# A one-core decoder layer: fewer side matmuls for denominators, first norm and HGRN2 row copies

## The chip, the cores and the metric

The kernel runs on one core of one Trainium2 chip. The metric is the device time of one execution in microseconds (us). Before the change the median of three runs was 2330.41 us (2330.23 to 2330.99).

## The reference

One layer of a decoder is computed for two groups of tokens that share the weights: one new sequence of 256 tokens, and 8 sequences of 8 tokens each that continue from a stored state (64 tokens). All 320 tokens go through every weight matrix together. In short:

```
proj = x @ w_in                      # 2048 -> 16392 columns
A: mLSTM, 4 heads:  s = (q k^T) * decay;  num = s v + q C0;  den = sum_s s + q n0
   h = num / max(|den|, exp(-m));  normalised per head
   C_new = decay * C0 + sum_s w_s k_s v_s^T
B: HGRN2, 8 heads:  o = (decayed q k^T) v + (q * decay) S0;  S_new = decay * S0 + sum_s k'_s v_s^T
x1 = LayerNorm(alpha*x + W_out(sig(ga)*A W_a + sig(gb)*B W_b))
y  = LayerNorm(alpha*x1 + relu(x1 W_up)^2 W_down)
```

Two sums matter here. `den` is a row sum of the score matrix, one number per token. The LayerNorm needs, for each token, the sum and the sum of squares over 2048 channels. And one update matters: for each of the 8 sample sequences, the state S of each HGRN2 head gets the sum over 8 tokens of a key row times a value row.

## The kernel before, in words

**Main stream.** Activations lie as channels x tokens: 16 blocks of 128 channels, 320 tokens wide. The weights are cut into 304 tiles of 2048 x 128. A tile is 16 steps, and each step is three matmuls, since each fp32 value is split into a high and a low fp32r part (high x high, high x low, low x high). That is 14592 matmuls of 320 columns. A half tile (512 KB, "unit") is loaded by SP into one of three raw buffers `wr`; ScalarE makes the high part (`wh`, line 331), VectorE the low part (`wl`, line 480), into three pairs of buffers; later tiles use five more pairs in `bb`.

**Side work.** Everything else is put between main steps by a planner that runs when the program is built. Pieces of work are Python generators ("chains") that yield (engine, cost, function). The planner keeps a clock for each engine; a PE piece is placed into TensorE's stream only once the planner believes that its operands are there (450 ns after the last of them, `PE_LAT`, and 140 ns more for a change of engine, `LAT`). A transfer costs SP 620 ns in the plan. The order is fixed then; on the chip each engine runs its own stream in order and waits on semaphores. So a wrong belief about a time turns into a wait of the whole stream behind that piece.

**The places that the change touches.**

- mLSTM scores (`m_S`, line 855) leave the masked scores of the prompt in the tile E, in three blocks of 128 columns; blocks 2 and 3 belong to the same 128 tokens. `m_num` (line 1008) sums them over s by matmuls with a column of ones, `one`, in fp32: one for the first 128 tokens, two that accumulate for the second. `m_sample` (line 1071) does the same for the sample tokens with three such matmuls: one over E, two over qn (q times the stored n0, two halves of the 256 channels).
- HGRN2 values (`h_i`, line 1374): the values of the 64 sample tokens are transposed, then split into a high part (partitions 64 to 127 of `vst`) and a low part (0 to 63). For the update each sequence needs its 8 rows four times, as high, high, low, low, at 32 partitions of its own. Two fp32r matmuls of 256 columns with a 0/1 matrix `spread` copy the rows into a PSUM bank, and ScalarE copies the bank back into `vst`.
- HGRN2 keys (`h_state`, line 1420): after a VectorE product, `stack` (line 915) writes high and low parts four times over into 256 columns (one ScalarE, one VectorE instruction), two transposes (line 1441) turn the two groups of 128 columns, and ScalarE copies them to `kst`.
- `h_update` (line 1469) waits for `vst`, takes four PSUM banks, issues eight matmuls of 32 rows x 256 columns, then eight VectorE instructions update the state tiles, and SP stores them. `hkst` and `hvst` are pools of one buffer, freed after the update.
- First LayerNorm (n = 0) and second (n = 1): `ln_sum` adds each block into S1 and its square into S2 on VectorE. After block 14 `ln_pre` (line 1717) starts two fp32 matmuls of a 128 x 128 matrix of ones with S1 and S2 (320 columns each); `ln_final` (line 1724) adds block 15 and its square to the same banks by two more.

**Order.** mLSTM heads 0 to 3 run in the first 440 us or so; the HGRN2 heads between about 440 and 850 us, one for each six tiles; then branches, output projection (16 tiles, the first norm at its end), and the feed-forward tiles. SP issues nearly all transfers in one in-order stream, the weight reloads among them.

Of the kernel before, what the change touches and what calls it, by code (L numbers as in the profile page):

```python
# [232 lines left out]
def wait(*evs):  # L233
    return ("wait", evs)
# [10 lines left out]
def post(ev):  # L245
    return ("set", ev)


def act(n, psum=False, ptr=0):
    return ((61 if psum else 112) + n) / 1.2 + 93 * ptr  # L250


def dve(n, psum=False, mode=1, ptr=0):
    return ((62 if psum else 66) + n / mode) / 0.96 + 55 * ptr
# [39 lines left out]
class Program:  # L294
# [48 lines left out]
    def carve(self):  # L343
        class Part:
            def __init__(self, ap, lo=0):
                self.ap, self.o, self.end = ap, lo, ap.shape[1]

            def __call__(self, n, parts=128):
                self.o += n
                assert self.o <= self.end, (self.o, self.end)  # L350
                return self.ap[:parts, self.o - n:self.o]

            def three(self, a, b):
                return self(a * b).rearrange("p (a b) -> p a b", a=a)

        self.Part = Part
        A, B, C, R = Part(self.f1), Part(self.f2), Part(self.f3), Part(self.ra[:, 0:6400])

        self.hs = Pool([A(2048) for _ in range(3)])

        self.qk = Pool([A.three(4, 320) for _ in range(2)])
        self.vr = Pool([A.three(4, 320)])
        self.kw = Pool([B.three(2, 320)])
        self.bc = Pool([B(712) for _ in range(2)])
        self.eb0 = B(512)
        self.eb = Pool([self.eb0])
        self.stg = Pool([B(256) for _ in range(2)])
        self.qn0 = B(256)
        self.qn = Pool([self.qn0])
        X = Part(self.rx)  # L370
        self.cb = Pool([C(512) for _ in range(6)] + [X(512) for _ in range(8)])
        self.hb = Pool([C.three(3, 512)])
        self.qz0 = C(512)
        self.qz = Pool([self.qz0])
        self.tst = Pool([B(320) for _ in range(2)])
        self.tst2 = B(320)
        self.shl = Pool([(R(384), R(384), R(256))])
        self.vhl = Pool([R(2048).rearrange("p (x s v) -> p x s v", x=2, s=2)])
        self.vs = Pool([R(512)])
        self.khl = Pool([R(1024).rearrange("p (x s k) -> p x s k", x=2, s=2)])  # L380
        self.kst = Pool([R.three(2, 256)])
        self.vst = Pool([R.three(2, 512)])

        A, B, R = Part(self.f1, 6144), Part(self.f2), Part(self.rh)
        self.sb = Pool([A.three(4, 256) for _ in range(2)])
        self.at = Pool([A(512) for _ in range(2)])
        self.yb0 = A(1024)
        self.yb = Pool([self.yb0])
        self.it2 = [B.three(3, 256) for _ in range(2)]
        self.it = Pool(self.it2)  # L390
        self.hstg = Pool([B(256) for _ in range(2)])
        self.on0 = B.three(3, 256)
        self.on = Pool([self.on0])
        self.ho = Pool([B(320) for _ in range(2)])
        R2 = Part(self.ra, 5120)
        self.hkst = Pool([R2.three(2, 128)])
        self.phl = Pool([(R2(512), R2(512))])
        self.hvst = Pool([R.three(2, 256)])
        self.late = [B(320) for _ in range(4)]
        self.ats0 = B(128)  # L400
        self.ats = Pool([self.ats0])
        self.sg = Pool([Part(self.f2, 4960)(320), self.tst2])
        B = Part(self.f2, 4304)
        self.sr = Pool([B(320) for _ in range(2)])
        B = Part(self.f2, 3840)
        self.xr = Pool([B(320) for _ in range(4)])
        B = Part(self.f2)
        self.lnb = [B(320) for _ in range(7)]
        self.tmp = Pool([B(320) for _ in range(3)])

    def carve_h(self):
# [3 lines left out]
        pp = C(512)  # L415
        self.pp = Pool([pp])
        self.ktk = Pool([C.three(2, 128)])
        for x in (qz, self.ats0, pp[:, 480:512], self.yb0[:, 320:384], *(y[64:128, 2, :] for y in self.it2)):
            self.nc.gpsimd.memset(x, 0.0)
        X, R = self.Part(self.pool.tile([128, 4096], F32R, name="rxb", tag="rx")), self.Part(self.ra)  # L420
        self.bah = Slices([(X if j < 12 else R)(TOK) for j in range(KT)])
# [436 lines left out]
    def m_S(self, h):  # L858
# [21 lines left out]
        yield ("dve", dve(384), lambda: v.tensor_tensor(sl, E[:, 0:384], f(sh), ALU.subtract))  # L880
        yield ("dve", dve(128), lambda: v.tensor_tensor(ss[64:128, 128:256], E[64:128, 384:512], f(ss[64:128, 0:128]), ALU.subtract))
        yield ("act", act(256), lambda: self.A(ss[0:64], f(ss[64:128])))
        yield post(m["S"])

    def m_V(self, h):
# [31 lines left out]
    def stack(self, st, src, his):  # L917

        v = self.nc.vector
        w = st.rearrange("p (b r t) -> p b r t", r=4, t=8)  # L920
        x = src.rearrange("p (b t) -> p b t", t=8).unsqueeze(2).to_broadcast([128, 8, 2, 8])
        step = his[1] - his[0]
        los = [r for r in range(4) if r not in his]
        pick = lambda rs: w[:, :, rs[0]:rs[0] + 2 * step - (step - 1):step, :]
        hi, lo = pick(his), pick(los)
        yield ("act", act(128), lambda: self.A(hi.bitcast(F32R), x))
        yield ("dve", dve(128), lambda: v.tensor_tensor(lo.bitcast(F32R), x, hi, ALU.subtract))

    def m_KW(self, h):
        nc, v, m = self.nc, self.nc.vector, self.mh[h]  # L930
# [78 lines left out]
    def m_num(self, h):  # L1009
# [9 lines left out]
        db = yield acq(self.sbank)  # L1019
        m["db"] = db  # L1020
        one = self.one
        yield ("pe", 212, lambda: self.mm(db[:, 0:1], E[:, 0:128], one, start=True, stop=True))
        yield ("pe", 212, lambda: self.mm(db[:, 1:2], E[:, 128:256], one, start=True, stop=False))
        yield ("pe", 212, lambda: self.mm(db[:, 1:2], E[:, 256:384], one, start=False, stop=True))
        for i in range(2):
            b = yield acq(self.sbank)
            jobs = [(c, s) for c, s in (((0, 0),), ((128, 0), (256, 1)))[i]]
# [50 lines left out]
    def m_sample(self, h):  # L1078
# [27 lines left out]
        for i in range(2):  # L1106
            yield ("pe", pe_r(512), lambda: self.mm(nb, ss[:, 128 * i:128 * i + 128], m["vs"], start=False, stop=i == 1, skip_group_check=True))
        db = yield acq(self.sbank)
        yield ("pe", 212, lambda: self.mm(db[:, 0:1], E[:, 384:512], self.one, start=True, stop=False))
        for c in range(2):  # L1110
            yield ("pe", 212, lambda: self.mm(db[:, 0:1], qn[:, 128 * c:128 * c + 128], self.one, start=False, stop=c == 1))
        dn = yield acq(self.sm)
        yield ("dve", 80, lambda: v.tensor_copy(dn[:, 0:1], db[:, 0:1]))
        yield rel(self.sbank, db)
# [81 lines left out]
    def h_start(self, h):  # L1196
# [2 lines left out]
        a = m["set"] = self.hs.free.pop(0)[1]  # L1199
        a = self.Part(a)  # L1200
        m["qk"], m["fs"], m["iv"] = a.three(2, 384), a.three(2, 320), a.three(2, 320)
        for n in ("f", "q", "lv", "o", "pre8", "suf", "I", "SP", "S", "aT", "qz", "ist", "sdone", "got", "ld"):
            m[n] = Ev()
        m["i"] = [Ev(), Ev()]
        m["Y"] = [Ev() for _ in range(5)]
# [165 lines left out]
    def h_i(self, h):  # L1371
# [22 lines left out]
        yield ("dve", dve(256, True), lambda: v.tensor_tensor(lo, b[64:128, 0:256], hi.bitcast(F32), ALU.subtract))  # L1394
        yield rel(self.sbank, b)
        yield post(m["I"])
        b = yield acq(self.sbank)
        bv = b.rearrange("p (g k) -> p g k", g=2)
        for g in range(2):
            yield ("pe", pe_r(256), lambda: self.mm(bv[:, g, :], self.spread[:, g, :], vst[:, 0, :], start=True, stop=True))  # L1400
        yield ("act", act(512, True), lambda: self.A(vst, bv))
        yield rel(self.sbank, b)
        yield post(m["ist"])

    def h_load(self, h):

# [13 lines left out]
    def h_state(self, h):  # L1420
# [10 lines left out]
            cap(qz, 0, [[136, 2], [32, 4], [1, 8]]), by_token(qk[:, 1, :], 256, False), by_token(fs[:, 1, :], 256, False), ALU.mult))  # L1431
        sm = yield acq(self.sm)
        yield ("dve", 80, lambda: v.tensor_copy(sm[:, 0:8], sv(fs[:, 1, :])[:, :, 7]))
        ks = fs[:, 0, 256:320]
        yield ("dve", dve(64), lambda: v.tensor_tensor(ks, qk[:, 0, 256:320], ks, ALU.mult))
        kst = yield acq(self.hkst)
        b = yield acq(self.sbank)
        st = yield acq(self.hstg)
        yield from self.stack(st, ks, (0, 2))
        for g in range(2):  # L1440
            yield ("pe", PE_T, lambda: nc.tensor.transpose(b[:, 128 * g:128 * g + 128], st[:, 128 * g:128 * g + 128], self.ident))  # L1441
        yield rel(self.hstg, st)
        yield ("act", act(256, True), lambda: self.A(kst, b[:, 0:256].rearrange("p (g k) -> p g k", g=2)))
        yield rel(self.sbank, b)
        ob = yield acq(self.sbank)
        m["ob2"] = ob
        yield wait(m["ld"])
# [21 lines left out]
    def h_update(self, h, kst, sm, e):  # L1469

        v, m = self.nc.vector, self.hh[h]
        yield wait(m["ist"])
        vst = m["vst"]
        ps = yield acq(self.sbank, 4)
        yield ("pe", PE_4 + 2 * pe_r(256), lambda: [self.mm(
# [192 lines left out]
    def ln_add(self, n, j, z, pre):  # L1668
# [29 lines left out]
            return  # L1698
        yield from self.ln_sum(j, z)
        yield post(st["s"][j])  # L1700
        if j == 14:
            self.s.spawn(self.ln_pre(n), 0)

    def ln_sum(self, j, z):
# [19 lines left out]
    def ln_final(self, n, z):  # L1724
# [3 lines left out]
        M, RS, X, T = (self.lnb[i] for i in (3, 4, 5, 6))  # L1728
        q = yield acq(self.tmp)
        t = yield ("act", act(TOK), lambda: self.A(q, z, AF.Square))  # L1730
        yield wait(st["pre"])
        p1, p2 = (p[:, :TOK] for p in st["p"])
        yield ("pe", pe_f(TOK), lambda: self.mm(p1, self.ones, z, start=False, stop=True))
        yield ("pe", pe_f(TOK), lambda: self.mm(p2, self.ones, q, start=False, stop=True))
        yield rel(self.tmp, q)
        yield post(st["fin"])
        t = yield ("act", act(TOK, True), lambda: self.A(M, p1, scale=1.0 / D))
# [122 lines left out]
    def run(self, pool):  # L1860
# [8 lines left out]
        self.vx, self.kx, self.main_end = Pool([]), Pool([]), Ev()  # L1869
        self.sD = [self.dr.tile([128, 768], F32, name=f"sD{j}") for j in range(HH)]  # L1870
        self.kD = [self.dr.tile([128, 2, 2, 256], F32, name=f"kD{j}") for j in range(MH)]
        self.vD = [self.dr.tile([128, 2, 2, 512], F32, name=f"vD{j}") for j in range(MH)]
        self.ln = [dict(c=Ev(), end=Ev(), pre=Ev(), m=Ev(), fin=Ev(), s=[Ev() for _ in range(KT)]) for _ in range(2)]
        self.xq, self.xq_ev = [None] * KT, [Ev() for _ in range(KT)]
# [80 lines left out]
```

## Time and profile before

The profiled execution took 2331.78 us; its span from first to last instruction is 2329.7 us.

| what | value |
|---|---|
| median of three runs | 2330.41 us |
| profiled execution, its span | 2331.78 us, 2329.7 us |
| PE (matmul) busy | 2314.0 us, 99% |
| weight loads into PE busy | 2266.9 us, 97% |
| VectorE (DVE) busy | 1381.1 us, 59% |
| ScalarE (ACT) busy | 1048.4 us, 45% |
| hardware DMA queue, share of 16 engines | 51.9% |
| mean granted TensorE clock | 0.999 |

PE is TensorE, DVE is VectorE, ACT is ScalarE, POOL is GpSimd, SP issues transfers. A group of the profile is named by line, engine, operation and tiles (out<-in). Most matmuls have line 337, because one helper issues them; they are told apart by their tiles. Matmuls are pipelined: a record can last about twice the distance between two starts, so costs on PE are read from the distance of starts, not from the length of records. "SPq" is SP's transfer stream.

### The profile page before, as it was taken

To read this page: it belongs to the slowest core of one execution; us is meant where nothing else is said; L and a number is where in the kernel's file an instruction comes from. 1 tells how busy PE (TensorE), PEld (TensorE's weight loads), DVE (VectorE), ACT (ScalarE), POOL (GpSimd) and SP (SyncE) were. 2 spreads that over 40 slices of the span, in tenths; PEclk is the share of its full clock that TensorE was granted. 3 is DMA by queue.
4 is the path that set the end of the run, shared out by engine and by line. 5 is a ranking of instruction groups with operands and counts; after the bars stand their busy time and mean duration, and the time that the engine had idled before them with its cause. 6 is when DMAs were issued, how large, how long until landed. Compare 5 with 4: busy or idle time off the path is not lost.

```text
span 2329.7 us, 38945 instructions
## 1 busy us (share of the span) xinstructions
PE 2314.0 (99%) x15746; PEld 2266.9 (97%) x15746; DVE 1381.1 (59%) x2400; ACT 1048.4 (45%) x1669; POOL 12.7 (1%) x42
## 2 busy tenths in 40 slices
PE   8999999999999999999999999999999999999998
PEld 7999999999999999999999999999999999999998
DVE  5566557677777776555555767544554455445555
ACT  4444445455555565444433446533442344334434
POOL 0000000000000000000000000000000000000000
PEclk9999999999999999999999999999999999999999
DMA  5777766555555554554555644444444444444465
GB/s 201 261 272 264 255 237 228 189 198 187 182 178 184 180 197 172 173 178 170 175 173 172 221 160 144 154 146 153 145 150 149 149 151 146 153 145 152 147 226 181
DMA packets 143580, 424.95 MB, mean 182 GB/s; under 512 B 16412, under 2 KB 37796, under 8 KB 142376
## 3 DMA queue, kind: packets, MB, share of 16 engines
q1 hardware_dynamic: 142248, 416.17, 51.9%
q0 software_dynamic: 1152, 6.29, 0.8%
q8 instruction: 123, 2.02, 0.4%
q14 instruction: 57, 0.47, 0.1%
HBM read 371.50 MB, written 50.90 MB: 181 GB/s over the span
## 4 chain that ended last, share of the span: by engine, by line
PE 97%; DMA 1%; DVE 1%; ACT 0%; issue 0%; SPq 0%; DVEq 0%; ACTq 0%
PE bank L337 96%; DMA wr<-wt 1%; DVE f3m L1844 0%; DVE f3m L1849 0%; PE bank L1553 0%; PE bank L899 0%; PE bank L1125 0%; DVE bb L480 0%; PE bank L1383 0%; ACT bb L331 0%; ACT wh L331 0%; DVE wl L480 0%; SPq L340 0%; PE bank L972 0%; PE bank L1441 0%
## 5 line engine op out<-in xcount | busy, mean ns | idle before, releaser
L480 DVE TENSOR_TENSOR wl<-wr,wh 128x1024 fp32r<-128x1024 f32 (+1 forms) x430 | 525.7, 1223 | 472.6 <-ACT wh L331 464.0
L337 PE MATMUL bank<-xh,wh 128*128 128x320 f32 (+1 forms) x2432 | 790.1, 325 | 0.9 <-ACT wh L331 0.9
L337 PE MATMUL bank<-xh,wl 128*128 128x320 f32 (+1 forms) x2432 | 754.3, 310 | 0.0
L337 PE MATMUL bank<-xl,wh 128*128 128x320 f32 (+1 forms) x2432 | 752.3, 309 | 0.0
L331 ACT ACTIVATE wh<-wr 128x1024 fp32r<-128x1024 f32 (+1 forms) x430 | 453.8, 1055 | 458.1 <-PE bank L337 433.0
L337 PEld LDWEIGHTS bank<-xh,wh 128*128 128x128 f32 x2432 | 458.7, 189 | 21.7 <-issue 15.0
L337 PEld LDWEIGHTS bank<-xl,wh 128*128 128x128 f32 x2432 | 459.5, 189 | 3.5
L337 PEld LDWEIGHTS bank<-xh,wl 128*128 128x128 f32 x2432 | 458.8, 189 | 0.2 <-DVE wl L480 0.2
L480 DVE TENSOR_TENSOR bb<-wr,bb 128x1024 fp32r<-128x1024 f32 x179 | 219.3, 1225 | 237.4 <-ACT bb L331 237.4
L337 PE MATMUL bank<-xh,bb 128*128 128x322 f32 x1280 | 287.2, 311 | 0.0
L337 PE MATMUL bank<-ra,bb 128*128 128x320 f32 x1264 | 283.8, 309 | 0.0
L331 ACT ACTIVATE bb<-wr 128x1024 fp32r<-128x1024 f32 x179 | 188.8, 1055 | 209.4 <-PE bank L337 198.0
L337 PE MATMUL bank<-rxb,bb 128*128 128x320 f32 x1112 | 255.4, 309 | 0.0
L337 PE MATMUL bank<-ra,wh 128*128 128x320 f32 x892 | 249.9, 309 | 0.0
L337 PEld LDWEIGHTS bank<-xh,bb 128*128 128x128 f32 x1280 | 215.9, 188 | 0.0
L337 PEld LDWEIGHTS bank<-ra,bb 128*128 128x128 f32 x1264 | 210.7, 188 | 0.4
L337 PE MATMUL bank<-xl,bb 128*128 128x322 f32 x640 | 198.7, 310 | 0.0
L337 PEld LDWEIGHTS bank<-rxb,bb 128*128 128x128 f32 x1112 | 188.5, 188 | 0.2
L331 ACT ACTIVATE f<-f,misc 128x320 f32<-128x320 f32 x210 | 118.1, 562 | 149.2 <-DVE f L1812 136.8
L337 PE MATMUL bank<-rxb,wh 128*128 128x320 f32 x596 | 184.3, 309 | 0.0
L337 PE MATMUL bank<-rxb,wl 128*128 128x320 f32 x596 | 183.9, 309 | 0.0
L337 PEld LDWEIGHTS bank<-ra,wh 128*128 128x128 f32 x892 | 161.6, 188 | 1.1 <-DVE ra L1583 0.9
(265 smaller groups left out, 2216.5 us busy)
## 6 DMA issues: line engine op xcount, KB each, us to landing
wr<-wt SPq DMA_DIRECT2D x607, 512.0 KB, 3.3
rx<-C SPq DMA_DIRECT2D x34, 256.0 KB, 6.0
Cs<-rx SPq DMA_DIRECT2D x34, 256.0 KB, 5.1
f<-C SPq DMA_DIRECT2D x30, 256.0 KB, 4.7
Cs<-f SPq DMA_DIRECT2D x30, 256.0 KB, 4.2
vD<-ra SPq DMA_DIRECT2D x4, 1024.0 KB, 8.7
f<-S SPq DMA_DIRECT2D x8, 512.0 KB, 5.5
f3h<-S SPq DMA_DIRECT2D x8, 512.0 KB, 6.2
```

What stands on the lines that cost most here:

```text
L331: return self.nc.scalar.activation(out, in_, func, **kw)
L337: self.nc.tensor.matmul(*a, **kw)
L480: self.V().tensor_tensor(lo[:, c], raw[:, c], hi[:, c].bitcast(F32), ALU.subtract)
```

## The change

Three sums are moved from matmul accumulation to VectorE adds, and the two HGRN2 copies of rows are made by transfers.

- `m_S` adds block 3 of E to block 2 (one VectorE add of 128 columns); `m_num` then needs one matmul for each 128 tokens. `m_sample` adds E and both halves of qn on VectorE (two adds) and needs one matmul.
- `ln_pre` is not run for n = 0; `ln_final` adds block 15 to S1 and its square to S2 on VectorE, and then issues the two matmuls from these sums.
- `h_state` transposes the key rows once (a 128-column staging tile with a zero half), and splits high and low on the way out of PSUM, as the values are. A new helper `copies` writes each high or low part of 64 rows to a DRAM tile four times (four transfers) and reads all 256 rows back into `kst` or `vst` (one transfer), for keys and values of each of the 8 heads.
- `h_update` waits for the keys' transfer as well. The planner is told to issue the read no earlier than 4000 ns after the last write's issue has ended, and takes the rows to be there 4500 ns after the read's issue has ended.

```diff
 m_S:
+        yield ("dve", dve(128), lambda: v.tensor_tensor(E[:, 128:256], E[:, 128:256], E[:, 256:384], ALU.add))
+    def copies(self, hi, lo, to, his, st, ev):
+        w = to.rearrange("(b r t) k -> r b t k", r=4, t=8)
+        for r in range(4):
+            t = yield ("sp", 620, lambda: self.dma(w[r], (hi if r in his else lo).bitcast(F32)))
+        t = yield ("sp", 620, lambda: self.dma(st.bitcast(F32), to.rearrange("(g p) k -> p g k", g=2)), (t + 4000.0,))
+        ev.t = t + 4500.0
 m_num:
-        yield ("pe", 212, lambda: self.mm(db[:, 0:1], E[:, 0:128], one, start=True, stop=True))
-        yield ("pe", 212, lambda: self.mm(db[:, 1:2], E[:, 128:256], one, start=True, stop=False))
-        yield ("pe", 212, lambda: self.mm(db[:, 1:2], E[:, 256:384], one, start=False, stop=True))
+        for i in range(2):
+            yield ("pe", 212, lambda: self.mm(db[:, i:i + 1], E[:, 128 * i:128 * i + 128], one, start=True, stop=True))
 m_sample:
-        yield ("pe", 212, lambda: self.mm(db[:, 0:1], E[:, 384:512], self.one, start=True, stop=False))
-        for c in range(2):
-            yield ("pe", 212, lambda: self.mm(db[:, 0:1], qn[:, 128 * c:128 * c + 128], self.one, start=False, stop=c == 1))
+        q0 = qn[:, 0:128]
+        yield ("dve", dve(128), lambda: v.tensor_tensor(q0, q0, E[:, 384:512], ALU.add))
+        yield ("dve", dve(128), lambda: v.tensor_tensor(q0, q0, qn[:, 128:256], ALU.add))
+        yield ("pe", 212, lambda: self.mm(db[:, 0:1], q0, self.one, start=True, stop=True))
 h_i:
-        b = yield acq(self.sbank)
-        bv = b.rearrange("p (g k) -> p g k", g=2)
-        for g in range(2):
-            yield ("pe", pe_r(256), lambda: self.mm(bv[:, g, :], self.spread[:, g, :], vst[:, 0, :], start=True, stop=True))
-        yield ("act", act(512, True), lambda: self.A(vst, bv))
-        yield rel(self.sbank, b)
-        yield post(m["ist"])
+        yield from self.copies(hi, lo, self.vsD[h], (0, 1), vst, m["ist"])
 h_state:
-        yield from self.stack(st, ks, (0, 2))
-        for g in range(2):
-            yield ("pe", PE_T, lambda: nc.tensor.transpose(b[:, 128 * g:128 * g + 128], st[:, 128 * g:128 * g + 128], self.ident))
-        yield ("act", act(256, True), lambda: self.A(kst, b[:, 0:256].rearrange("p (g k) -> p g k", g=2)))
+        yield ("pe", PE_T, lambda: nc.tensor.transpose(b[:, 0:128], st, self.ident))
+        hi, lo = kst[64:128, 0, :], kst[0:64, 0, :]
+        yield ("act", act(128, True), lambda: self.A(hi, b[64:128, 0:128]))
+        t = yield ("dve", dve(128, True), lambda: v.tensor_tensor(lo, b[64:128, 0:128], hi.bitcast(F32), ALU.subtract))
+        self.s.spawn(self.copies(hi, lo, self.ksD[h], (0, 2), kst, m["kst"]), 4, t)
 h_update:
-        yield wait(m["ist"])
+        yield wait(m["ist"], m["kst"])
 ln_add:
-        if j == 14:
+        if j == 14 and n:
             self.s.spawn(self.ln_pre(n), 0)
 ln_final (n = 0):
+            yield ("dve", dve(TOK), lambda: v.tensor_tensor(S1, S1, z, ALU.add), (t - act(TOK) - LAT,))
+            yield ("dve", dve(TOK), lambda: v.tensor_tensor(q, S2, q, ALU.add), (t,))
+            st["p"] = yield acq(self.sbank, 2)
```

More of the change, by code (lines that the diff above doesn't have):

```diff
@@ L390, in carve @@
         self.it = Pool(self.it2)
-        self.hstg = Pool([B(256) for _ in range(2)])
+        self.hstg0 = [B(128) for _ in range(2)]
+        self.hstg = Pool(self.hstg0)
         self.on0 = B.three(3, 256)
@@ L417, in carve_h @@
         self.ktk = Pool([C.three(2, 128)])
-        for x in (qz, self.ats0, pp[:, 480:512], self.yb0[:, 320:384], *(y[64:128, 2, :] for y in self.it2)):
+        for x in (qz, self.ats0, *(x[:, 0:64] for x in self.hstg0), pp[:, 480:512], self.yb0[:, 320:384], *(y[64:128, 2, :] for y in self.it2)):
             self.nc.gpsimd.memset(x, 0.0)
@@ L1201, in h_start @@
         m["qk"], m["fs"], m["iv"] = a.three(2, 384), a.three(2, 320), a.three(2, 320)
-        for n in ("f", "q", "lv", "o", "pre8", "suf", "I", "SP", "S", "aT", "qz", "ist", "sdone", "got", "ld"):
+        for n in ("kst", "f", "q", "lv", "o", "pre8", "suf", "I", "SP", "S", "aT", "qz", "ist", "sdone", "got", "ld"):
             m[n] = Ev()
@@ L1433, in h_state @@
         yield ("dve", 80, lambda: v.tensor_copy(sm[:, 0:8], sv(fs[:, 1, :])[:, :, 7]))
-        ks = fs[:, 0, 256:320]
-        yield ("dve", dve(64), lambda: v.tensor_tensor(ks, qk[:, 0, 256:320], ks, ALU.mult))
+        st = yield acq(self.hstg)
+        yield ("dve", dve(64), lambda: v.tensor_tensor(st[:, 64:128], qk[:, 0, 256:320], fs[:, 0, 256:320], ALU.mult))
         kst = yield acq(self.hkst)
         b = yield acq(self.sbank)
-        st = yield acq(self.hstg)
-        yield from self.stack(st, ks, (0, 2))
-        for g in range(2):
-            yield ("pe", PE_T, lambda: nc.tensor.transpose(b[:, 128 * g:128 * g + 128], st[:, 128 * g:128 * g + 128], self.ident))
+        yield ("pe", PE_T, lambda: nc.tensor.transpose(b[:, 0:128], st, self.ident))
         yield rel(self.hstg, st)
-        yield ("act", act(256, True), lambda: self.A(kst, b[:, 0:256].rearrange("p (g k) -> p g k", g=2)))
+        hi, lo = kst[64:128, 0, :], kst[0:64, 0, :]
+        yield ("act", act(128, True), lambda: self.A(hi, b[64:128, 0:128]))
+        t = yield ("dve", dve(128, True), lambda: v.tensor_tensor(lo, b[64:128, 0:128], hi.bitcast(F32), ALU.subtract))
         yield rel(self.sbank, b)
+        self.s.spawn(self.copies(hi, lo, self.ksD[h], (0, 2), kst, m["kst"]), 4, t)
         ob = yield acq(self.sbank)
@@ L1730, in ln_final @@
         t = yield ("act", act(TOK), lambda: self.A(q, z, AF.Square))
-        yield wait(st["pre"])
+        if n:
+            yield wait(st["pre"])
+        else:
+            S1, S2 = self.lnb[0], self.lnb[1]
+            yield ("dve", dve(TOK), lambda: v.tensor_tensor(S1, S1, z, ALU.add), (t - act(TOK) - LAT,))
+            yield ("dve", dve(TOK), lambda: v.tensor_tensor(q, S2, q, ALU.add), (t,))
+            st["p"] = yield acq(self.sbank, 2)
         p1, p2 = (p[:, :TOK] for p in st["p"])
-        yield ("pe", pe_f(TOK), lambda: self.mm(p1, self.ones, z, start=False, stop=True))
-        yield ("pe", pe_f(TOK), lambda: self.mm(p2, self.ones, q, start=False, stop=True))
+        yield ("pe", pe_f(TOK), lambda: self.mm(p1, self.ones, z if n else S1, start=n == 0, stop=True))
+        yield ("pe", pe_f(TOK), lambda: self.mm(p2, self.ones, q, start=n == 0, stop=True))
         yield rel(self.tmp, q)
@@ L1871, in run @@
         self.kD = [self.dr.tile([128, 2, 2, 256], F32, name=f"kD{j}") for j in range(MH)]
+        rows = lambda name, n, k: [self.dr.tile([32 * NB, k], F32, name=f"{name}{j}") for j in range(n)]
+        self.ksD, self.vsD = rows("ksD", HH, HK), rows("vsD", HH, HV)
         self.vD = [self.dr.tile([128, 2, 2, 512], F32, name=f"vD{j}") for j in range(MH)]
```

## The prediction

> **What bounds the kernel now.** I read the page's chain of waits first, then the waits of PE, then PE's groups by shape, then PE's timeline, and last the transfers of the HGRN2 stage. The chain:
>
> ```profile
> PE 97%; DMA 1%; DVE 1%; ACT 0%; issue 0%; SPq 0%; DVEq 0%; ACTq 0%
> ```
>
> Almost all of the chain that ends last is TensorE. All that PE ever waited for is:
>
> ```profile
> PE bank L337 <- DVE ra L681: 4.3, 1, 4.3
> PE bank L337 <- ACT xh L331: 2.1, 1, 2.1
> PE bank L337 <- DVE f L1678: 0.9, 1, 0.9
> PE bank L337 <- ACT wh L331: 0.9, 1, 0.9
> PE bank L337 <- DVE xl L676: 0.3, 1, 0.3
> ```
>
> That is 8.5 us: 6.7 at the start (lines 676, 681, `xh`), 1.8 near 1310 us. In the HGRN2 stage there is none; the table by stretches (PE, weight loads, DVE, ACT, POOL, clock, DMA share, GB/s) says so as well:
>
> ```profile
> 440.00:850.00 410.00, 410.00 (x2880) 397.61 (x2879) 305.13 (x797) 218.25 (x444) 2.86 (x9) 1.00 0.55 186
> ```
>
> PE is busy 410.00 of 410 us at full clock. So an instruction taken off PE's stream is worth what it takes there, until something makes PE wait. VectorE (74%) and the transfers (0.55) have room.
>
> **What leaves PE.** The groups that lose instructions (count, busy time, mean):
>
> ```profile
> L337 PE MATMUL bank<-misc,f 128*128 128x1 f32 x48 | 6.6, 208 | 0.0
> L337 PE MATMUL bank<-rh,ra 128*128 128x256 f32 x16 | 4.6, 289 | 0.0
> L1441 PE MATMUL bank<-cst,f 128*128 128x128 f32 x16 | 4.3, 272 | 0.0
> L337 PE MATMUL bank<-f,ones 128*128 128x320 f32 x16 | 5.7, 438 | 0.9 <-DVE f L1678 0.9
> ```
>
> Their means are lengths of pipelined records and too large. The price is what one inserts between main matmuls. A transpose in the timeline (start, length):
>
> ```profile
> 498.26 0.31 PE L337 MATMUL bank<-xh,wl 128*128 128x320 f32 x1
> 498.41 0.27 PE L1441 MATMUL bank<-cst,f 128*128 128x128 f32 x1
> 498.44 0.39 PE L337 MATMUL bank<-xh,wh 128*128 128x320 f32 x1
> 498.67 0.31 PE L337 MATMUL bank<-xl,wh 128*128 128x320 f32 x1
> ```
>
> From `xh,wl` to the second main matmul after it takes 498.67 - 498.26 = 0.41 us; undisturbed, the same distance is 499.55 - 499.26 = 0.29. So a transpose costs 0.12 us, not 0.27. The others in the same way:
> - a spread matmul, 501.89 to 502.31: 0.42 - 0.29 = 0.13;
> - a denominator matmul (a pair of records, so 24 matmuls in the group of 48), 193.00 to 193.51: 0.51 - 0.29 = 0.22;
> - a norm matmul (also a pair), 1390.16 to 1390.99: 0.83 - 0.29 = 0.54.
>
> Removed: 4 heads x (1 + 2) = 12 denominator matmuls, 12 x 0.22 = 2.64; 8 x 2 = 16 spread matmuls, 16 x 0.13 = 2.08; 8 transposes, 8 x 0.12 = 0.96; 2 norm matmuls, 2 x 0.54 = 1.08. The sum is 6.8 us. By the groups' busy time it would be 3.3 + 4.6 + 2.2 + 1.4 = 11.5; I hold that for an upper end, since it counts overlap.
>
> The Trainium skill speaks against the largest term: "TensorE: Matmul & The Clock Gate", section "Back-to-back issue gap", gives an isolated matmul of 1 to 64 columns a floor of about 25 ns. By that the 12 x 2 records would be worth 0.6 us and the sum 4.7. The timeline has 0.22 us for a pair, so the row decides; the weight load of 128 columns goes with each record, and that page's section "LDWEIGHTS" (columns / 1.2 ns, so 107 ns) agrees with the row.
>
> **What is added beside PE.** VectorE gets 12 adds of 128 columns (the 128x128 add of line 1276 takes 284 ns) and two of 320 (line 1713: 489 ns): 4.4 us over the run. The key rows trade a 128x128 ACT and DVE instruction and a 128x256 ACT copy for a 64x128 copy and subtraction out of PSUM (between the 0.22 us of the 128x64 PSUM copy of line 1360 and the 381 and 426 ns of the 64x256 ones), and a 128x512 ACT copy of 594 ns falls away per head. So ACT and DVE gain in that stage. All of it lies beside PE, and PE's waits above show this cover; without it, the 12 adds would cost 3.4 us, the two of the norm 1.0. The denominators' adds stand ahead of matmuls that the planner places only after them, so nothing queues there.
>
> The first norm's end moves later by the adds. VectorE stands idle 2.00 us before its weight instruction at 1398.79, so the next `xl` (1399.93) need not move. The norm's results are used first at 1408.47, for a bank that PE needs again only when five further tiles of 7.1 us have begun, about 1429.6. I cost it at nothing; uncovered it is 1.0 us.
>
> Queues: SP gets 8 x 2 x 5 = 80 issues of 0.33 to 0.43 us (gbD, sD and S issues in its timeline), some 30 us of 410, in a stream that mostly waits. POOL gets two small memsets, with no one behind them. Packets: 16 x (256 + 256) = 8192 more; at the mean packet (51.9% x 16 x 2329.7 / 142248 = 0.136 us) that is at most 70 us of an engine's time over the stage, so the share goes from 0.55 to 0.72 at most. The stretch 0 to 350 us ran at 0.71, with PE's only waits in its first 10 us.
>
> **The wait that is added.** `h_update`'s eight matmuls now wait for rows that go to DRAM and back. Behind them in PE's stream stands the main stream, so each us that the rows come late is a us lost, 8 times. Up to now `kst` and `vst` came from ACT; the update at 655.1 would move to about 663, which by itself costs nothing: the next head's rows come 50 us later, long after the single buffers are free. The plan allows a write 0.62 + 4.0 + 0.14 = 4.8 us from its issue to the read's, and a read 0.62 + 4.5 + 0.14 + 0.45 = 5.7 us to the matmul. No such transfer exists yet. The nearest rows of that stage (size, median us from issue to landing):
>
> ```profile
> gbD<-f SPq DMA_DIRECT2D x12, 160.0 KB, 2.1
> oT<-f SPq DMA_DIRECT2D x16, 160.0 KB, 2.7
> f<-hT SPq DMA_DIRECT2D x8, 160.0 KB, 3.7
> sD<-f SPq DMA_DIRECT2D x8, 256.0 KB, 4.9
> f3h<-S SPq DMA_DIRECT2D x8, 512.0 KB, 6.2
> ```
>
> The writes are 32 and 64 KB, four in a row; the reads 128 and 256 KB. A write lies between 2.1 and 4.9 us, a read between 3.3 (the weight loads) and 6.2. I take 2.7 and 4.5: between `hT` and `S`, whose two loads of 512 KB go out together and wait for each other. Then nothing is late. At the far ends 0.1 + 0.5 = 0.6 us is late per head, 4.8 us in all.
>
> The Trainium skill ("DMA: Bandwidth & Descriptors", "Anatomy of one DMA") counts 2.0 us plus bytes / 436 GB/s for one transfer, measured on GpSimd's path: estimates of 2.2 us for a write of values and 2.6 for their read, no lateness. The row of `S` (6.2 for 512 KB, where that rule gives 3.2) shows how far sharing stretches it, so I keep the row's end for a rival.
>
> **Sum.** Against the profiled execution: 2331.78 - 6.8 = 2325.0. It lies 1.4 us above the median, so the forecast is 2330.4 - 6.8 = 2323.6.
>
> **Rivals.**
> - *Rows slightly late.* Writes and reads take the slowest rows: 8 x 0.6 = 4.8 us back, 2328.4. For it: no PE piece follows so soon on a transfer in the old program. Against: the rows are smaller than those of 4.9 and 6.2.
> - *Reads behind the state loads.* This one ends slower. At 657.03 SP issues two S loads for the next head, just where the reads are due. If they are ahead, a read lands after their 6.2 us plus its own share: the S loads move 1 MB in about 6.2 - 2.1 = 4.1 us, the 384 KB of both reads take 1.5 more. It is late by 6.2 + 1.5 - 5.7 = 2.0 us, times 8 = 16, minus 6.8: 2339.6. It decides from (6.8 + 4.7) / 8 = 1.4 us per head. Against: by the plan the reads are due about 1 us before these loads.
> - *No gain.* PE's freed time comes back as waits for weights, since ACT, DVE and transfers feed it: 2330.4. Against: in 410 us it waited for none, and its reloads wait for DVE, not DVE for them.
>
> **Chances and range.** What a measurement of this kernel can tell from no change is about 0.2%, 4.7 us. Forecast 0.64, slightly late 0.18, behind the loads 0.12, no gain 0.06. So faster 0.64, same 0.24, slower 0.12. The forecast alone spans 2321.9 to 2325.3: 38 prices read to 0.02 us (0.8 us), and one more or one fewer wait like the 0.9 us ones near 1310 us, since the planner's order shifts. With the late and no-gain cases the range reaches 2331.0, and leaves out the slower rival and a little below.
>
> **What would show it.** In the profile after: the four groups at 24, 0, 8 and 14 records, and `f3m,ones` at 2 instead of 4 (in the first norm two pairs are left of four, beside the one at block 3); PE's waits still near 8.5 us; update matmuls about 8 us later in each head, with no idle time ahead. Wrong would be a wait of PE on a DMA into `rh` or `ra` eight times over 0.2 us, a wait on weights behind SP's reads, or a new wait at the first norm.

## The result, and the profile after

The changed kernel takes 2324.74 us (median of 9 runs, 2322.81 to 2325.97), the kernel before 2330.99 us in the runs beside it (2330.23 to 2333.91). The ratio is 0.9971, 95% interval 0.996 to 0.9981: 6.3 us, or 0.29%, faster. In a later set of runs (`after_same`, below) it was 0.9969 (0.9956 to 0.9981). The profiled execution went from 2331.78 to 2324.84 us, its span from 2329.7 to 2323.0.

PE is still what ends last. The page's chain of waits after the change, shares of the span by engine:

```profile
PE 97%; DMA 1%; DVE 1%; ACT 0%; SPq 0%; issue 0%; DVEq 0%
```

The four groups that were to lose instructions, and the norm's matmuls over its blocks (`f3m`), after the change (count, busy time, mean | idle before):

```profile
L337 PE MATMUL bank<-f,ones 128*128 128x320 f32 x14 | 5.0, 439 | 0.4 <-DVE f L1684 0.4
L337 PE MATMUL bank<-rh,ra 32*128 32x256 f32 x64 | 4.1, 327 | 1.7 <-DMA ra<-ksD 1.7
L337 PE MATMUL bank<-misc,f 128*128 128x1 f32 x24 | 3.3, 208 | 0.0
L1444 PE MATMUL bank<-cst,f 128*128 128x128 f32 x8 | 2.2, 272 | 0.0
L337 PE MATMUL bank<-f3m,ones 128*128 128x320 f32 x2 | 0.7, 432 | 0.0
```

The spread matmuls (`rh,ra` of 128x256) are gone; the counts are 24, 8, 14 and 2, as predicted. The line `rh,ra 32x256` is the state update, and it has something that it had not before: 1.7 us of idle time, ended by a transfer. All of PE's waits after the change:

```profile
PE bank L337 <- DVE ra L682: 4.3, 1, 4.3
PE bank L337 <- ACT xh L331: 1.9, 1, 1.9
PE bank L337 <- DMA ra<-ksD: 1.7, 2, 1.2
PE bank L337 <- ACT wh L331: 0.7, 1, 0.7
PE bank L337 <- DVE ra L906: 0.4, 1, 0.4
PE bank L337 <- DVE f L1684: 0.4, 1, 0.4
PE bank L337 <- DVE xl L677: 0.3, 1, 0.3
```

The waits at the start are the old ones (7.2 us where they were 7.6), and the one near 1310 us went from 0.9 to 0.4. The prediction puts 1.8 us near 1310; in the trace of before only the 0.92 us on `f` stand there (1311.35), and the 0.86 us on `wh` stand at the start (5.92). The 0.4 us on line 906, at 66 us, aren't the change's doing: `norm` and `spread9` below, which alter nothing there, have 0.5 and 0.4 us at the same transposes. What the change added is the wait on `ra<-ksD`. It stands twice (1.2 and 0.5 us): PE waits for the keys' rows on their way back from DRAM. The stretch of the HGRN2 heads:

```profile
440.00:850.00 410.00, 408.30 (x2862) 395.60 (x2861) 306.62 (x795) 214.79 (x431) 2.87 (x9) 1.00 0.61 203
```

PE is busy 408.30 of 410 us where it was 410.00: the missing 1.7 us are those two waits. VectorE's time there grows by 1.5 us, ScalarE's falls by 3.5 us, and the share of the transfers goes from 0.55 to 0.61.

Where do the two waits come from? SP's stream in the first of the two heads (start, length, transfer):

```profile
500.69 1.82 SPq L340 DMA_DIRECT2D ksD<-ra  x3
502.55 0.93 SPq L340 DMA_DIRECT2D f<-S  x2
503.59 0.38 SPq L340 DMA_DIRECT2D rh<-vsD  x1
...
506.72 0.38 SPq L340 DMA_DIRECT2D ra<-ksD  x1
```

And the two transfers in the chain of waits (start, duration):

```profile
506.72 7.10 DMA ra<-ksD
659.20 6.16 DMA ra<-ksD
```

The keys' read is issued 4.2 us behind two state loads of 512 KB, and takes 7.1 us to land. PE came to the update at about 512.8 (it starts at 513.96 after 1.18 us of idle time), 6.1 us after the read's issue. The second, at 659.20, has the state loads at 655.07 ahead of it in the same way.

The times at which the trace's semaphores were raised give the landing of the keys' read in all eight heads:

| head | keys' read issued, us | state loads of the next head issued from, us | landed after, us | PE waited, us |
|---|---|---|---|---|
| 0 | 454.24 | 451.23, ahead of it | 5.5 | 0 |
| 1 | 506.72 | 502.55, ahead of it | 7.1 | 1.2 |
| 2 | 557.24 | 553.40, ahead of it | 5.2 | 0 |
| 3 | 600.73 | 603.33 | 2.5 | 0 |
| 4 | 659.20 | 655.07, ahead of it | 6.2 | 0.5 |
| 5 | 700.03 | 704.36 | 3.3 | 0 |
| 6 | 747.45 | 755.39 | 2.1 | 0 |
| 7 | 799.98 | none | 2.3 | 0 |

Behind the loads a read took 5.2 to 7.1 us, elsewhere 2.1 to 3.3. In heads 0 and 2 PE came to the update only 7.0 and 7.7 us after the read's issue, so those reads cost nothing.

### The profile page after: what moved, and what is told of

Read it like the earlier page. It is cut to its first block, busy times and chain, and to the rows that moved or that the text cites. A ratio compares the mean times of both kernels' runs of the same rounds, so it can differ in the third digit from the quotient of the medians.

```text
span 2323.0 us, 38948 instructions
## 1 busy us (share of the span) xinstructions
PE 2306.7 (99%) x15694; PEld 2259.7 (97%) x15694; DVE 1385.8 (60%) x2414; ACT 1042.9 (45%) x1653; POOL 12.9 (1%) x44
## 4 chain that ended last, share of the span: by engine, by line
PE 97%; DMA 1%; DVE 1%; ACT 0%; SPq 0%; issue 0%; DVEq 0%
PE bank L337 96%; DMA ra<-ksD 1%; DVE f3m L1861 0%; DVE f3m L1856 0%; PE bank L1137 0%; PE bank L1559 0%; PE bank L902 0%; DMA wr<-wt 0%; DMA f<-scr 0%; ACT f L331 0%; SPq L340 0%; PE bank L1395 0%; ACT wh L331 0%; PE bank L983 0%; PE bank L1400 0%
```

## The experiments

**Theory A** is the prediction's: PE's stream is the bound; an instruction taken from it is worth the time that it inserts between main matmuls; the adds and transfers lie beside; only a late row costs, and it costs what PE waits. **Rivals:** the price is the busy time of the records (B), or an issue floor (C); VectorE's adds cost (D); the rows are late in themselves, wherever their reads are issued (E).

### The three parts, one at a time

`den` has only the denominators' edits of the diff, `norm` only those of `ln_add` and `ln_final`, `copies` only those of `h_i`, `h_state`, `h_update` and the helper.

> Only the denominators' part of the change: 12 fp32 matmuls of one column fewer, 12 VectorE adds more. Theory (price = what one inserts between main matmuls, 0.22 us; adds hidden): -2.6 us, PE busy down by 2.6. Rival by busy time of the records (0.275 us a pair of records): -3.3 us. Rival by an issue floor of 25 ns a record: -0.6 us. Rival that VectorE's adds cost: above the kernel before. No wait of PE on VectorE at the denominators.

> Only the first norm's part: 2 fp32 matmuls of 320 columns fewer, 2 VectorE adds more. Theory: -1.1 us, and no new wait of PE in the first feed-forward tiles. Rival (the later end of the norm holds the first feed-forward tiles): 0 or slower, with a wait of PE between 1390 and 1430 us.

> Only the HGRN2 row copies through DRAM; denominators and norm as before. Theory: 16 spread matmuls and 8 transposes fewer, -3.0 us, and up to 1.7 us of PE's waits on the keys' rows back, so -1.3 us or a little more, with waits only in heads whose read is issued behind the state loads. Rival (rows are late in most heads): 0 or slower.

| kernel | median us | before beside it | ratio, 95% interval | PE's waits on rows |
|---|---|---|---|---|
| den | 2327.82 | 2330.82 | 0.9987 (0.9978 to 0.9996) | none |
| norm | 2329.68 | 2330.82 | 0.9996 (0.9987 to 1.0005) | none |
| copies | 2327.50 | 2330.82 | 0.9985 (0.9977 to 0.9994) | none |

The parts give -3.0, -1.1 and -3.3 us, where A had -2.6, -1.1 and -1.3 to -3.0. The time of `den` doesn't tell A's price from B's (-3.3), and the norm's gain can't be told from nothing; no new wait stands at the first feed-forward tiles in its trace, only the one at block 3 of the norm (near 1310 us), 1.5 us here and 0 to 1.9 us in the traces of all these kernels. `copies` is a miss in a useful way: I expected PE's two waits here as well, and there were none over 0.1 us, so the whole price of the removed matmuls stayed. The reads stand behind the state loads in the same four heads; in heads 1 and 4 they landed 6.0 and 5.8 us after issue, and the updates start 6.1 and 5.9 us after it. So a difference of about 1 us in the landing decides whether PE waits. The sum of the three, -7.4, lies within the interval of the whole (-9.3 to -4.4).

### The price of an instruction, by adding many

`den9` is the kernel before with 24 more denominator matmuls in each of the two places of each head, 192 in all; `spread9` issues each spread matmul nine times, 128 more.

```diff
 m_num, and in the same way m_sample:
+        for _ in range(24):
+            yield ("pe", 212, lambda: self.mm(db[:, 0:1], E[:, 0:128], one, start=True, stop=True))
 h_i:
+            for _ in range(9):
                 yield ("pe", pe_r(256), lambda: self.mm(bv[:, g, :], self.spread[:, g, :], vst[:, 0, :], start=True, stop=True))
```

> The kernel before, with 192 more denominator matmuls (24 for each head in both places, results overwritten by the true ones): the price of one. Theory 0.22 us each: +42 us, 2373. By the busy time of a pair of records, 0.275 us: +53 us, 2383. By an issue floor of 25 ns for each of two records: +10 us, 2340.

> The kernel before, with each spread matmul ninefold: 128 more. Theory 0.12 to 0.13 us each: +15 to +17 us, 2346 to 2347. By the busy time of the group, 0.289 us: +37 us, 2367.

`spread9` took 2346.37 us beside 2330.78, ratio 1.0067 (1.0052 to 1.0082): 15.6 / 128 = 0.122 us each. That is A's price and not B's 0.289. `den9` took 2377.94, ratio 1.0199 (1.0184 to 1.0214): 47.2 us, between A's 42 and B's 53, far from C's 10. Its trace shows that it is A's. One such pair between main matmuls:

```profile
92.82 0.30 PE L337 MATMUL bank<-xh,wl 128*128 128x320 f32 x1
92.96 0.28 PE L337 MATMUL bank<-misc,f 128*128 128x1 f32 x2
93.10 0.40 PE L337 MATMUL bank<-xh,wh 128*128 128x320 f32 x1
93.33 0.32 PE L337 MATMUL bank<-xl,wh 128*128 128x320 f32 x1
```

93.33 - 92.82 = 0.51, less the undisturbed 0.29: 0.22 us, as in the kernel before. 192 of them are 42.2 us. From one profiled execution to the other the span grew by 45.8 us (2329.7 to 2375.5), and PE's waits by 3.3 of these (8.5 to 11.8; the two on line 903 are 2.5). Without the waits 42.5 us are left, 0.22 us for each of the 192. The price is A's.

### VectorE's adds

`adds8` keeps every matmul of the kernel before and puts 8 times the added VectorE work into the same places, into a spare tile.

```diff
 m_S:
+        for _ in range(8):
+            yield ("dve", dve(128), lambda: v.tensor_tensor(self.spare[:, 0:128], E[:, 128:256], E[:, 256:384], ALU.add))
 m_sample:
+        for _ in range(16):
+            yield ("dve", dve(128), lambda: v.tensor_tensor(self.spare[:, 128:256], qn[:, 0:128], E[:, 384:512], ALU.add))
```

> The kernel before, with eight times as many VectorE adds at the denominators as the change adds (96 adds of 128 columns, 27 us of VectorE, into a spare tile), and every matmul kept. Theory (adds hidden beside PE): within 0.5 us of the kernel before, 2331. Rival (they stand on the way to the end): up to +27 us.

It took 2330.79 us beside 2330.78, ratio 1.0001 (0.9991 to 1.001). 96 adds cost nothing that can be measured, so 12 don't either. D falls for the denominators.

### The order of the key reads and the state loads

`hold` issues a head's state loads, from the third head on, only behind both row reads of the head before; `behind` does the opposite and issues the keys' read of heads 0 to 6 only behind the next head's state loads.

```diff
 hold, h_load:
+        if h > 1:
+            yield wait(self.hh[h - 1]["vout"], self.hh[h - 1]["kout"])
 behind, copies (keys only):
+        if nxt:
+            yield wait(nxt["ld"])
```

> The change, with one order altered: the state loads of a head from the third on are issued only after both row reads of the head before. Theory (the two waits of 1.2 and 0.5 us come from reads issued behind state loads): no wait of PE on the keys' rows is left and the time falls by up to 1.7 us below the changed kernel, to about 2323. Rival (the reads are late in themselves, through their 512-byte rows): the waits stay and the time is that of the changed kernel, 2324.7. Third possibility: the state loads become late themselves and PE waits on them.

> The changed kernel again, on the chip of the next three, so that they can be compared. Theory: 2324.7 as before, with PE's waits on the keys' rows (1.7 us in the first profile) in heads whose read stands behind the state loads, and nowhere else.

> The kernel with the state loads held back, again, on the same chip as the changed kernel. Theory: lower than the changed kernel by what PE waits there on the keys' rows, 1 to 2 us. Rival (the difference of 1.6 us between the first two was one of chips): equal within 0.5 us.

> The change, with one order altered the other way: in heads 0 to 6 the keys' read is issued only behind the next head's two state loads. Theory by the prediction's rival: the read lands about 7.7 us after its issue where the plan allows 5.7, so PE waits some 2 us in each of 7 heads, 14 us, and the time is about 2338. By the first profile (four reads behind the loads, waits of 1.2 and 0.5 us in two of them): about 0.4 to 1.2 us a head, 3 to 8 us, so 2326 to 2331. If the order doesn't matter: 2324.7.

`hold` took 2323.08 us beside 2330.82, ratio 0.9967 (0.9954 to 0.9979). On one chip, with a common median of 2331.03 for the kernel before:

| kernel | median us | ratio, 95% interval | PE's waits on the keys' rows |
|---|---|---|---|
| changed (`after_same`) | 2323.28 | 0.9969 (0.9956 to 0.9981) | 1.2 us, 1 place |
| `hold_same` | 2322.76 | 0.9967 (0.9954 to 0.9979) | none |
| `behind` | 2326.57 | 0.998 (0.9972 to 0.9989) | 2.6 us, 4 places |

PE's waits follow the order as A says. SP's stream of `hold` in the head that waited 1.2 us before:

```profile
507.57 0.38 SPq L340 DMA_DIRECT2D ra<-ksD  x1
508.00 0.54 SPq L340 DMA_DIRECT2D sD<-f  x1
508.58 1.91 SPq L340 DMA_DIRECT2D f<-S  x2
```

Now the read stands ahead of the loads, and the update at 513.51 starts 5.9 us after it with no wait. By the semaphores it landed 4.0 us after its issue. The seven reads of this trace that don't stand behind the loads took 2.1 to 4.0 us, the one that does (head 0) 6.2. So the rows aren't late in themselves, and E falls. In `behind` the reads in the chain:

```profile
606.31 7.65 DMA ra<-ksD
705.82 8.52 DMA ra<-ksD
757.44 7.83 DMA ra<-ksD
```

These three, 7.7 to 8.5 us, are the longest; all seven reads behind the loads took 5.0 to 8.5, so the rival's 7.7 is near their upper end. But PE waits only 2.6 us in all, not 14: it comes to the update 6.1 to 7.7 us after the read's issue, where the prediction had 5.7. What holds the update back (the four banks that it needs, or another order of the plan) the runs don't show. `behind` is 3.3 us slower than the changed kernel, of which the waits explain 1.4; the rest is not settled. The time alone does not tell `hold_same` from the changed kernel: I expected 1 to 2 us, and the 0.5 us measured lies within the intervals. That the held order removes the waits on the rows is shown; that it makes the kernel faster is not.

### A late row, made on purpose

`early` lets the planner believe that the rows are there before the read's issue has ended.

```diff
 copies:
-        ev.t = t + 4500.0
+        ev.t = t - 500.0
```

> The change, but the planner believes the rows to be there 0.5 us before the read's issue has ended, in place of 4.5 us after it, so that the update matmuls stand about 5 us earlier in PE's stream. Theory (behind a late row stands the whole main stream): PE waits on the rows in nearly all 8 heads, some 2 to 5 us each, 16 to 35 us in all, and the time grows by what PE waits: about 2340 to 2358. Rival (PE's waits are made up elsewhere): within 2 us of the changed kernel, 2324.7.

It took 2347.79 us beside 2330.78, ratio 1.0071 (1.0056 to 1.0086). PE's waits:

```profile
PE bank L337 <- DMA ra<-ksD: 16.4, 4, 5.5
```

Four heads, not eight, but 2.5 to 5.5 us in each. They are the four whose keys' read stands behind the state loads here: it landed 5.6 to 7.0 us after its issue, in the other four 2.6 to 3.1. The profiled execution took 2344.05 us, 19.2 more than that of the changed kernel, while the waits on the rows are only 14.7 more. Most of the other 4.5 us can be seen in PE's timeline after the waits; after the longest:

```profile
461.25 0.80 PE L337 MATMUL bank<-rh,ra 32*128 32x256 f32 x8 [5.50 <-DMA ra<-ksD]
462.42 0.47 PE L337 MATMUL bank<-xl,wh 128*128 128x320 f32 x1
462.69 0.47 PE L337 MATMUL bank<-xh,wl 128*128 128x320 f32 x1
```

`xl,wh` to `xh,wl` takes 0.27 us, where 0.15 is usual. The stretches around it (after PE, weight loads, DVE, ACT and POOL comes the granted clock):

```profile
455.00:460.00 5.00, 0.75 (x6) 0.49 (x4) 1.94 (x4) 1.06 (x1) 0.00 (x0) 1.00 1.00 345
460.00:465.00 5.00, 3.75 (x21) 3.52 (x22) 2.91 (x8) 0.42 (x2) 0.00 (x0) 0.66 0.19 74
465.00:470.00 5.00, 5.00 (x33) 4.73 (x32) 0.80 (x4) 1.81 (x4) 0.00 (x0) 1.00 0.28 113
```

The clock is 0.66 in the stretch in which PE starts again, and the matmuls stay slow until about 464.2, some 3 us, of which about 1.3 are lost (3 x 0.12 / 0.27, an estimate). The clock is 0.66 as well in the stretches after the waits of 3.76 and 4.56 us (572 to 577, 627 to 632); three times 1.3 us is about 4 of the 4.5. So a long wait costs more than its length. The wait of 2.53 us in this kernel (update at 520.17) leaves the clock at 1.00. The first of the three stretches shows what the read runs into: while PE waits, the transfers' share is 1.00.

### The same copies for the mLSTM heads

Since the held kernel was the best, `mrows` adds to it the same copies for the 4 mLSTM heads: 8 spread matmuls of 512 columns and 8 transposes fewer.

```diff
 m_V:
-        for g in range(2):
-            b = yield acq(self.sbank)
-            yield ("pe", pe_r(512), lambda: self.mm(b, self.spread[:, g, :], vs, start=True, stop=True))
-            yield ("act", act(512, True), lambda: self.A(vst[:, g, :], b))
-            yield rel(self.sbank, b)
-        yield post(m["vst"])
+        yield from self.copies(vs[64:128], vs[0:64], self.vmD[h], (0, 1), vst, m["vst"], Ev())
```

> The kernel with the state loads held back, and the same copies through DRAM for the mLSTM's sample rows: 8 fp32r spread matmuls of 512 columns (0.24 us each between main matmuls) and 8 transposes (0.11) fewer. Theory: -2.8 us against the held kernel, about 2320.3, if no row is late; the mLSTM stage moves more data (share 0.71 before). Rival (transfers of that stage are slower, 4.2 to 6 us for 256 KB): PE waits on rows in some of 4 heads and half or all of the gain goes.

It took 2339.93 us, ratio 1.004 (1.0026 to 1.0053): slower than the kernel before, and 17.2 us slower than `hold_same` on the same chip, where I expected 2.8 us less. PE's largest wait:

```profile
PE bank L337 <- DMA ra<-kmD: 10.9, 3, 5.2
```

Three waits (3.6, 2.1 and 5.2 us), of the rival's kind, and worse than it: more than the gain was lost. In the chain a keys' write there takes 4.06 us to land and the read that waits for it 3.99; and SP issued the fourth write only at 359.53, 3.8 us after the third (355.77), since the values' read stood in its stream in between and waited for writes. The share of the transfers in 0 to 440 us is 0.73.

The waits don't make up the whole loss. The clock falls here too, to 0.50, 0.66 and 0.51 in the five us in which each wait ends, also after the shortest:

```profile
275.44 0.51 PE L337 MATMUL bank<-ra 32*128 32x512 f32 x4 [2.13 <-DMA ra<-kmD]
275.00:280.00 5.00, 4.56 (x21) 4.31 (x22) 1.61 (x4) 1.06 (x1) 0.00 (x0) 0.66 0.89 265
```

That wait is shorter than the one of 2.53 us in `early`, after which the clock stayed at 1.00. So the length of the wait alone doesn't decide; what else does, these runs don't show.

## Why the prediction held, and where it was off

**The bound, and what leaves PE: right.** Instructions off PE's stream are worth what they insert there. Spread matmul: 0.13 predicted, 0.122 measured. Denominators: 0.22, and 0.22 again in `den9`. The Trainium skill's floor of 25 ns for a matmul of one column ("TensorE: Matmul & The Clock Gate", "Back-to-back issue gap") would have made `den9` about 10 us slower, an estimate (192 x 2 x 25 ns); it was 47.

**The adds beside PE: right**, shown by `adds8` for the denominators. For the norm the trace shows no new wait; its 1.1 us can't be told from nothing. I had said that VectorE gains in the HGRN2 stage; it has 1.5 us more to do there, and that cost nothing.

**The added wait: the step that was off, by 1.7 us.** I took 4.5 us for a read, and nothing late. No keys' read took that: it was 2.1 to 3.3 us, or 5.2 to 7.1 behind the state loads, and I had the reads due ahead of these loads, which failed in four of eight heads. In two of them PE waited. The rival that named this place was right on the mechanism; its landing, 7.7 us, lies above the changed kernel's and inside the 5.0 to 8.5 of `behind`; and its price was wrong, 2.0 us in each head, against 0 to 1.2. Two things were not in it: half of the reads don't stand behind the loads, and PE often comes to the update later than the 5.7 us that I allowed. The updates themselves moved by 4.4 to 10.4 us, where I had about 8.

The Trainium skill's formula in "DMA: Bandwidth & Descriptors" ("Anatomy of one DMA"), 2.0 us plus bytes / 436 GB/s, gives an estimate of 2.3 us for the keys' read of 128 KB. That agrees with the 2.1 to 3.3 us of the reads that don't stand behind the loads; behind 1 MB of loads it was 5.2 to 7.1.

**The sum: closer than its terms, by luck.** The forecast, 2323.6, is 1.1 us below the 2324.74 measured. Between the two profiled executions PE's waits grew by 1.2 us, to which the sum gave nothing, and the span without them fell by 7.8 us (2321.1 to 2313.3), to which it gave 6.8. The two misses nearly cancel. Where the extra 1.0 us comes from is open: it is less than the runs of one kernel differ by.

**SP's issues: mis-sized, without effect.** I took 0.33 to 0.43 us for an issue, some 30 us in all. The writes of 64 rows take 0.58 each at the median (578 ns for keys, 581 for values), the reads 0.38, so 64 x 0.58 + 16 x 0.38 = 43 us. The share of the transfers rose to 0.61, below the bound of 0.72.

**"No gain"** fell: the weights were never late in the HGRN2 stage.

## What to carry to other kernels

Where one engine is busy all the time, price an instruction by the distance that it opens between its neighbours' starts, not by its record's length: here 0.12 against 0.29 us. A copy through DRAM that takes work off that engine is free only as long as the plan puts its reads ahead of large loads in the queue and the consumer behind their real landing; `mrows` shows how fast an expected gain of 2.8 us turns into a loss of 17.2 against the same held kernel. Look for the transfers that happen to be issued beside the new one, since they set its latency here: 2.1 to 3.3 us without them ahead, 5.2 to 7.1 behind them.

## What was not expected of the hardware

A wait of TensorE of 5.5 us cost more than its length: the granted clock was 0.66 in the five us from 460 on, and 0.51 around a wait of 5.2 us in `mrows`. One of 2.53 us left it at 1.00, but one of 2.13 us in `mrows` was followed by 0.66. The Trainium skill ("TensorE: Matmul & The Clock Gate", Part 1) says that an idle window of about 3.4 us halves the clock until the array has been busy about as long. The second half agrees with these traces (matmuls 0.27 us apart in place of 0.15, for some 3 us); the first does not in one place, where the wait ahead of the slow clock was only 2.13 us. And a write of 64 rows of 512 bytes or 1 KB occupied SP's stream for 0.58 us at the median, SP's other transfers of that stage for 0.33 to 0.44 (medians of the groups).
